# Sixteen-kilobyte runs and 4 MB loads for streamed expert weights

## The chip, the cores and the metric

The kernel runs on one core of a Trainium2 chip. The metric is the device time of one execution in microseconds (us). A core has the engines PE (TensorE), DVE (VectorE), ACT (ScalarE), POOL (GpSimd) and SP (SyncE), and 16 DMA engines that move data from the device memory to the core's own memory of 128 partitions.

## The reference, cut to what matters

One layer of a decoder for 256 tokens and 1024 channels: a mixer of three branches, then a feed-forward part of 32 experts of which each token takes four. The experts:

```python
def moe_ffn(h, router_w, router_b, w_gu, b_gu, w_down, b_down):
    logits = (t @ router_w + router_b).astype(jnp.float32)
    top_vals, top_idx = lax.top_k(logits, TOP_K)            # 4 of 32
    gate_w = jax.nn.softmax(top_vals, axis=-1)
    ...
    def expert_block(args):
        xb, e = args
        gu = xb @ w_gu[e] + b_gu[e]                         # w_gu[e]: 1024 x 2048, float32
        gate, up = jnp.split(gu, 2, axis=-1)
        gate = jnp.minimum(gate, SWIGLU_LIMIT)
        up = jnp.clip(up, -SWIGLU_LIMIT, SWIGLU_LIMIT)
        glu = gate * jax.nn.sigmoid(SWIGLU_ALPHA * gate)
        return ((up + 1.0) * glu) @ w_down[e] + b_down[e]   # w_down[e]: 1024 x 1024, float32
```

All weights are float32 and every expert is used: 268 MB of gate/up weights and 134 MB of down weights, each read once.

## The kernel before, in words

The mixer takes the first 335 us of the profiled execution, the routing some 9 us, and the experts nearly all of the rest. Experts are worked on in 16 pairs, 0 to 15. The tokens of a pair lie in the 128 columns of the array, in four groups of 32, so one product with a block of weights is four matmuls of 32 columns (`tiles4`, L1286 in the profile), which take their weights as the moving operand.

For pair p PE does gate/up p first, in eight blocks of 128 input channels (`gate_up`), and then down p-1 (`down`). Between blocks stand the scatter of an earlier pair's result (L1276), the gather of the next pair's tokens (L1121), and at the end of gate/up a bias product (L1303) and the transposes of the activations (`transpose_act`, L1253). The last pair is written out by itself (`ahead`, `meanwhile`): down 14, a branch on whether some expert has more tokens than slots (PE's sequencer at L1393), and down 15, cut in small pieces so that its last products and the final norm come late by little.

Weights come by one stream. All loads stand in one list (`add`) in the order of their use, and SP issues them in that order with `nc.sync.dma_start` (`load`, L159). They land in a ring of seven buffers of 2 MB (`ringp`, 16 KB on each partition); three loads of the first two pairs go to buffers that the mixer no longer needs (`EXTRA`). `issue` emits as many loads as fit the ring; `passed` says that a buffer's weights are used up. A load that takes a used buffer waits for the last matmul that reads it.

One load of gate/up is 2 MB: one block of 128 rows for both experts of the pair, 8 KB in one run to each partition, in one DMA. One load of down is 2 MB in two DMAs of 1 MB, one for each expert: two blocks of 128 rows, 4 KB in one run. Partition p holds row k * 128 + p of block k, so the channels of a block are 128 neighbours. Down 14 and 15 are loaded by columns, in pieces of 512 and 256 (runs of 2 KB and 1 KB).

Of the kernel before, what the change touches and what calls it, by code (L numbers as in the profile page):

```python
# [19 lines left out]
P = 128  # L20
# [29 lines left out]
class Carve:  # L50
    """Consecutive column ranges of a tile."""
# [11 lines left out]
class Turn:  # L63
    """Operands taken in turn."""
# [11 lines left out]
def trunk(ctx: ExitStack, tc: tile.TileContext, x, c, norm1_g, ada_w, ada_b, w_in, gmlp_norm_g, gmlp_ws,  # L76
# [6 lines left out]
    ringp = ctx.enter_context(tc.tile_pool(name="ring", bufs=RING))  # L83
# [31 lines left out]
    loads, got = [], []  # L115
    free_now = {}

    def add(fn, where=None):
        loads.append((fn, where))
        return len(loads) - 1  # L120

    def issue(n):
        """Emits the loads that fit while load n is in use and earlier ones are not."""
        while len(got) < len(loads):
            i = len(got)
            fn, where = loads[i]
# [14 lines left out]
    def chunk(n):  # L141
        """Load n; earlier ones are not used any more, but for those that are held."""
        last[0] = max(n, last[0])
        issue(min(held | {last[0]}))
        assert loads[n][1] or sum(loads[j][1] is None for j in range(n, len(got))) <= RING
# [3 lines left out]
    def passed(n):  # L149
        """Load n and those before it are not used any more."""  # L150
# [24 lines left out]
    def add_ada1(q):  # L175
        """Columns q*256 .. of shift1 and scale1."""
# [7 lines left out]
    def add_ada23(j):  # L184
        """512 columns of gate1, shift2, scale2, gate2."""
# [40 lines left out]
    EXTRA = {(0, KB - 1): "rest", (1, KB - 2): "b2", (1, KB - 1): "b4"}  # L226

    def add_gu(p, k):
        src = wgu[2 * p:2 * p + 2, k * P:(k + 1) * P, :].rearrange("e p n -> p e n")
# [7 lines left out]
        gu_ids[p, k] = add(fn, EXTRA.get((p, k)))  # L237

    def add_dn(p, *slots):
        """Loads of the pair's rows k0 .. k0 + k, columns c0 .. c0 + n, several to a slot."""  # L240
        dn_ids[p] = []

        def fn(t, parts):
            off = 0
            for k0, k, c0, n in parts:
                for e in range(2):
                    load(blocks(t, k, n, off=off), rows_of(wdn[2 * p + e], k0, k, c0, n))
                    off += k * n
        for parts in slots:
            i = add(lambda t, parts=parts: fn(t, parts))  # L250
# [5 lines left out]
    for p in range(NP):  # L256
        for k in range(KB):
            if (p, k) not in EXTRA or p == 0:
                add_gu(p, k)
            if (p, k) == (0, 3):  # L260
# [3 lines left out]
        if p:  # L264
            add_dn(p - 1, *([[(2 * q, 2, 0, D)] for q in range(4)] if p < NP - 1 else
# [4 lines left out]
    # ------------------------------------------------------------------ what stays  # L270
# [4 lines left out]
    vec2 = keep.tile([P, 64], F32, name="vec2")  # L275
    C_, N1, A1 = 0, 8, 16
    GG, PS_, CW, N2, A2 = 0, 8, 16, 40, 48
# [20 lines left out]
    vrow1, vrow2 = b4(P, rows=32), b4(P, rows=64)  # L298
# [3 lines left out]
    # -- loads that come before the stream  # L302
# [4 lines left out]
    def late_loads():  # L307
# [3 lines left out]
        vrows(vrow2, N2, norm2_g[0])  # L311
        vrows(vrow2, A2, ada_b[0, 3 * D:5 * D])
        load(wsr, gmlp_ws[0].rearrange("h t s -> t h s"))
        load(bsr, gmlp_bs.rearrange("o h t -> o (h t)"))
        load(rw, router_w[0].rearrange("(k p) e -> p k e", p=P))
# [16 lines left out]
    def rstd(r, m, w, table=False):  # L332
        """r = m ** -0.5, w columns (eps is in m), polished by a Newton step."""
# [9 lines left out]
    def table(f):  # L343
        """Has function f's table on the engine ahead of its use."""
# [5 lines left out]
    # ================================================================== token mixer  # L350
    # -- x's statistics and c
# [20 lines left out]
    def turn_x(b):  # L372
        """Blocks 2b and 2b + 1 of the normed rows, turned channel-major."""
# [7 lines left out]
    # -- conditioning: products by channel, summed over the partitions by a product with ones  # L381
# [10 lines left out]
    def weigh_rows(acc, w, k, first=False):  # L392
        """acc (+)= row block k of w times the conditioning."""
# [5 lines left out]
    def weigh_tiles(ps, w, i):  # L399
        """Products of the conditioning and w: row block g + 4i added in each of rows 32g .. 32g + 31, i = 0, 1."""  # L400
# [10 lines left out]

    def to_sums(acc, by):
        """Sums over the partitions that by picks: columns b * 128 .. of them in each of rows 32b .. 32b + 31."""
        ps = bbank()
        for b in range(4):
            TE.matmul(ps[b * GRP:(b + 1) * GRP, :P], lhsT=by[:, :1].to_broadcast([P, GRP]), rhs=acc[:, b * P:(b + 1) * P], start=True, stop=True)
# [26 lines left out]
    def h_block(kk):  # L443
        """Block kk of h, channel-major, as an exact pair."""
# [16 lines left out]
    def pair3(out_, ws, xs_, first, last_):  # L461
        """out_ += ws x xs_ for pairs (hi, lo) of both, without lo x lo (below float32's last bit)."""
# [7 lines left out]
    def col_item(name, m, pair, evac):  # L470
        """128 columns of a weight, channel-major."""
# [19 lines left out]
    def row_step(get, kk, banks, pair, evac, before=None):  # L491
        """One block of rows times 512 columns, token-major."""
# [22 lines left out]
    def later(k, fn):  # L515
        """Has fn emitted k steps later."""
# [5 lines left out]
    # -- v: gelu, root mean square over the channels  # L522
# [33 lines left out]
    # -- u, first with half of the channels, then with the rest  # L556
# [31 lines left out]
    def spatial_setup():  # L588
        """Spatial weights, transposed and causal; their bias on every partition; the other vectors."""
# [24 lines left out]
        def vectors():  # L614
            ps[2] = bbank()
            TE.transpose(ps[2][:, :64], vrow2, ident[:64, :64])

        def to_vec2():
            V.tensor_copy(vec2, ps[2][:, :64])
# [6 lines left out]
    def shift_scale(q, *between):  # L626
        """The rows of products, their sums by channel, and other steps after each."""
# [8 lines left out]
    def v_steps(q, *parts):  # L636
        """Columns c2 of row block k for parts (c2, k)."""
# [20 lines left out]
    # -- the spatial gate  # L658
# [17 lines left out]
    class Act:  # L676
        """The operand pair of the projections, made when the first part of it is."""
# [14 lines left out]
    # -- the other two thirds of the conditioning, a row block at a time between the steps  # L692
# [3 lines left out]
    def ada23(j):  # L696
# [27 lines left out]
        def cols_evac():  # L724
            u = 4 * (j - 2)
            V.tensor_tensor(mod2[:, u:u + 4], cell["pc"], vec2[:, A2 + u:A2 + u + 4], op=OP.add)
# [5 lines left out]
            if j == 5:  # L732
                V.scalar_tensor_tensor(a2, mod2[:, KB:], 1.0, vec2[:, N2:N2 + 8], op0=OP.add, op1=OP.mult)
# [16 lines left out]
    def gate_bias(j):  # L750
        """Rows of zeros, but for the bias on the first partition."""
# [19 lines left out]
    # -- gates and the first projection  # L771
# [739 lines left out]
```

## Time and profile before

| | us |
|---|---|
| median of 3 runs | 1311.47 |
| lowest, highest | 1308.33, 1312.13 |
| span of the profiled execution | 1308.2 |
| PE busy in it | 1201.0 |

The profiled execution is told by its span, from the first to the last instruction; what lies around the span is not in the trace, and the lowest of the runs stands at the span within 0.2 us. A timeline row has the start and the length of a group of equal instructions in us, then engine, line, operation, output and input, count, and in brackets the idle time before and what ended it. L1286 is line 1286 of the kernel. `SPq` rows are DMA issues on SP. `PEclk` is the share of TensorE's full clock that was granted, and the DMA share is the mean busy share of 16 DMA engines by their packets' time, which can come out a little above 1. 484.75 MB are moved in the whole execution.

### The profile page before, as it was taken

The numbers are of one execution on the slowest core, as the hardware profiler recorded it, in microseconds if no ns is written. First come the engines' busy times: TensorE is split into PE (matmuls) and PEld (weight loads), VectorE is DVE, ScalarE is ACT, GpSimd is POOL, SyncE is SP. The second block draws the span as 40 slices with busy tenths as digits, with TensorE's granted clock in tenths as the row PEclk, the third lists the DMA queues.
The fourth block names the chain that finished last, engine by engine and source line by source line (L and its number), as shares of the span: only waits on it lengthen the run. The fifth ranks groups of instructions, "written<-read, shape, count | busy, mean of one in ns | idle before, by whom it ended". The sixth has DMA issues, their size and how long they took to land. (4 is left out here: it accounts for less than half of the span.)

```text
span 1308.2 us, 22663 instructions
## 1 busy us (share of the span) xinstructions
PE 1201.0 (92%) x9653; PEld 603.3 (46%) x9654; DVE 440.1 (34%) x884; ACT 270.6 (21%) x538; POOL 11.0 (1%) x27
## 2 busy tenths in 40 slices
PE   7999999999899999999897999898888989898867
PEld 5899998999533333333232333232323323232222
DVE  3477886877431121311112221212111111212022
ACT  5564554555321010100000010100000000001002
POOL 0010000000000000000000000000000000000001
PEclk9999999999999999999999999999999999999989
DMA  9996487776999999999999999999999999999993
GB/s 344 340 387 223 179 293 292 264 277 264 329 390 368 418 417 414 420 413 420 413 421 413 420 414 418 417 416 418 414 420 414 420 414 418 416 419 416 387 366 117
DMA packets 121014, 484.75 MB, mean 371 GB/s; under 512 B 6601, under 2 KB 21033, under 8 KB 88398
## 3 DMA queue, kind: packets, MB, share of 16 engines
q1 hardware_dynamic: 120230, 481.52, 92.6%
q10 hardware_dynamic: 680, 1.71, 0.4%
q8 instruction: 81, 1.33, 0.4%
q14 instruction: 23, 0.19, 0.0%
HBM read 482.16 MB, written 1.05 MB: 369 GB/s over the span
## 5 line engine op out<-in xcount | busy, mean ns | idle before, releaser
L1286 PE MATMUL abank<-wchunk,b 128*32 (+2 forms) x4160 | 478.1, 592 | 52.9 <-DMA wchunk<-in_exp_w_down_dram 41.8
L1286 PEld LDWEIGHTS abank<-wchunk,b 128*32 128x32 f32 x4160 | 135.8, 110 | 359.9 <-issue 356.6
L1286 PE MATMUL cbank<-wchunk,b 128*32 128x512 f32 (+2 forms) x1952 | 231.9, 593 | 14.6 <-DMA wchunk<-in_exp_w_gu_dram 14.6
L1058 DVE TENSOR_SCALAR b<-bbank,a,mod 128x128 f32<-128x128 f32 x64 | 26.2, 410 | 398.6 <-PE bbank L1121 398.6
L458 DVE TENSOR_TENSOR spl<-wchunk,spl 128x512 fp32r<-128x512 f32 x196 | 132.2, 691 | 49.0 <-ACT spl L457 46.1
L1056 ACT ACTIVATE b<-bbank,mod,a 128x128 f32<-128x128 f32 x64 | 29.2, 457 | 540.5 <-PE bbank L1121 540.5
L457 ACT ACTIVATE spl<-wchunk 128x512 fp32r<-128x512 f32 x196 | 120.8, 627 | 76.3 <-PE abank L468 46.5
L465 PE MATMUL abank<-b,spl 128*128 128x256 f32 x432 | 110.3, 287 | 0.0
L466 PE MATMUL abank<-b,spl 128*128 128x256 f32 x432 | 108.3, 283 | 0.0
L1121 PEld LDWEIGHTS bbank<-spl,b 128*128 128x128 f32 x512 | 65.6, 191 | 91.2 <-issue 89.3
L1286 PEld LDWEIGHTS cbank<-wchunk,b 128*32 128x32 f32 x1952 | 51.6, 109 | 117.6 <-issue 85.9
L1121 PE MATMUL bbank<-spl,b 128*128 128x128 f32 x512 | 86.3, 298 | 2.0 <-DVE spl L1114 0.9
L465 PEld LDWEIGHTS abank<-b,spl 128*128 128x128 f32 x432 | 82.7, 192 | 3.5 <-issue 2.4
L1339 DVE TENSOR_TENSOR row<-abank,x 128x512 f32<-128x512 f32 (+1 forms) x32 | 21.9, 683 | 182.7 <-PE abank L1286 182.7
L466 PEld LDWEIGHTS abank<-b,spl 128*128 128x128 f32 x432 | 82.8, 192 | 0.2 <-issue 0.2
L1218 DVE TENSOR_TENSOR xt<-bbank,xt 128x512 f32<-128x512 f32 (+1 forms) x66 | 44.6, 676 | 106.0 <-PE bbank L1276 105.9
L468 PE MATMUL abank<-b,spl 128*128 128x256 f32 x432 | 69.7, 283 | 0.0
L1276 PE MATMUL bbank<-row,b 128*128 128x512 f32 (+1 forms) x132 | 62.7, 605 | 1.6 <-DVE row L1339 1.4
L468 PEld LDWEIGHTS abank<-b,spl 128*128 128x128 f32 x432 | 59.8, 192 | 0.0
L465 PE MATMUL cbank<-b,spl 128*128 128x256 f32 x224 | 57.2, 287 | 0.0
L466 PE MATMUL cbank<-b,spl 128*128 128x256 f32 x224 | 56.2, 283 | 0.0
L1269 ACT ACTIVATE b<-bbank 128x256 f32<-128x256 f32 x16 | 6.1, 383 | 237.5 <-PE bbank L1267 237.5
(272 smaller groups left out, 839.0 us busy)
## 6 DMA issues: line engine op xcount, KB each, us to landing
wchunk<-in_exp_w_gu_dram SPq DMA_DIRECT2D x125, 2048.0 KB, 22.9
wchunk<-in_exp_w_down_dram SPq DMA_DIRECT2D x122, 1024.0 KB, 27.0
wchunk<-in_w_in_dram SPq DMA_DIRECT2D x16, 2048.0 KB, 9.6
wchunk<-in_ada_w_dram SPq DMA_DIRECT2D x8, 2048.0 KB, 19.7
wchunk<-in_ada_w_dram SPq DMA_DIRECT2D x16, 512.0 KB, 14.7
wchunk<-in_exp_w_down_dram SPq DMA_DIRECT2D x10, 512.0 KB, 9.1
wchunk<-in_w_in_dram SPq DMA_DIRECT2D x4, 1024.0 KB, 10.1
wchunk<-in_w_proj_a_dram SPq DMA_DIRECT2D x2, 2048.0 KB
```

Source lines behind the costliest of these rows:

```text
L457: S.activation(hi, w, AF.Copy)
L458: V.tensor_tensor(lo, w, hi.bitcast(F32), op=OP.subtract)
L465: TE.matmul(out_, lhsT=wh, rhs=xh, start=first and i == 0, stop=False)
L466: TE.matmul(out_, lhsT=wh, rhs=xl, start=False, stop=False)
L468: TE.matmul(out_, lhsT=wl, rhs=xh, start=False, stop=last_ and i == n - 1)
L1056: S.activation(out_, in_, AF.Identity, scale=a2[:, k:k + 1], bias=sh2[:, k:k + 1])
L1058: V.tensor_scalar(out_, in_, a2[:, k:k + 1], sh2[:, k:k + 1], op0=OP.mult, op1=OP.add)
L1121: TE.matmul(ps, lhsT=xn2[:, tt, k * P:(k + 1) * P], rhs=oh[p][:, tt].rearrange("p a g -> p (a g)"), start=tt == 0, stop=tt == TT - 1)
L1218: V.tensor_tensor(xt[:, tt, s], ps, xt[:, tt, s], op=OP.add)
L1276: TE.matmul(ps, lhsT=wt[:, tt * P:(tt + 1) * P], rhs=wk["yv"][:, c:c + n], start=True, stop=True)
L1286: TE.matmul(out_[g * GRP:(g + 1) * GRP], lhsT=xl[:, g * GRP:(g + 1) * GRP], rhs=w(e), start=start, stop=stop, skip_group_check=True)
L1339: V.tensor_tensor(wk["yv"][:, c:c + m], bank[c], wk["g2b"][:, c:c + m], op=OP.mult)
```

## The change

A partition takes neighbouring rows of a weight: two of gate/up, four of down, 16 KB in one run of the device memory. The input channels of a block are then every second, or every fourth, channel, and all that meets the weights is read to match: the transposes of the activations take every fourth column, the transposes and sums of the mixer's result every second (`of_block`), the copies of the normed rows and the loads of three vectors and of the router's weights are reordered.

The ring is one buffer of seven units of 2 MB. Loads of gate/up and down are 4 MB, in two DMAs of 2 MB (one for each expert), and go to units 0 and 1, 2 and 3, or 4 and 5; unit 6 takes loads of 2 MB only: the mixer's, single blocks of the first two pairs, down 14 and 15. `lay` fixes beforehand which units a load takes, those whose last load is the oldest, and `issue` emits a load once all loads before it in its units are passed.

```diff
-    ringp = ctx.enter_context(tc.tile_pool(name="ring", bufs=RING))
+    ringp = ctx.enter_context(tc.tile_pool(name="ring", bufs=1))
...
+    ring = ringp.tile([P, RING * CHUNK_ELEMS], F32, name="wchunk")
...
+    def lay():
+        first = next(i for i, (_, _, size) in enumerate(loads) if size == 2)
+        turn = -sum(where is None for _, where, _ in loads[:first]) % RING
+        of = [-RING + (u - turn) % RING for u in range(RING)]
+        for i, (_, where, size) in enumerate(loads):
+            if where is not None:
+                place.append((None, ()))
+                continue
+            u = min(range(0, RING - size + 1, size), key=lambda u: max(of[u:u + size]))
+            place.append((u, tuple(j for j in of[u:u + size] if j >= 0)))
+            of[u:u + size] = [i] * size
...
             if where is None:
-                if sum(loads[j][1] is None for j in range(n, i)) >= RING:
+                u, before_it = place[i]
+                if any(j >= n for j in before_it):
                     return
-                t = ringp.tile([P, CHUNK_ELEMS], F32, name="wchunk")
+                t = ring[:, u * CHUNK_ELEMS:(u + size) * CHUNK_ELEMS]
...
-    EXTRA = {(0, KB - 1): "rest", (1, KB - 2): "b2", (1, KB - 1): "b4"}
+    EXTRA = {(0, KB - 2): None, (0, KB - 1): "rest", (1, KB - 2): "b2", (1, KB - 1): "b4"}
...
+    def add_gu2(p, j):
+        def fn(t):
+            v = t.rearrange("p (e m) -> p e m", e=2)
+            for e in range(2):
+                load(v[:, e], wgu[2 * p + e, 2 * j * P:2 * (j + 1) * P, :].rearrange("(p i) n -> p (i n)", i=2))
+        n = add(fn, None, 2)
+        for i in range(2):
+            gu_ids[p, 2 * j + i] = (n, i)
...
-            add_dn(p - 1, *([[(2 * q, 2, 0, D)] for q in range(4)] if p < NP - 1 else
+            add_dn(p - 1, *([[(4 * j, 4, 0, D)] for j in range(2)] if p < NP - 1 else
                             [[(k, 4, c, 512)] for c in (0, 512) for k in (0, 4)]))
...
-            S.activation(xn2[:, tt, half(h)], xt[:, tt, half(h)], AF.Copy, scale=r2[:, tt:tt + 1])
+            S.activation(xn2[:, tt, half(h)].rearrange("p (j i q) -> p j i q", j=2, i=2),
+                         xt[:, tt, half(h)].rearrange("p (j q i) -> p j i q", j=2, i=2), AF.Copy, scale=r2[:, tt:tt + 1])
...
-                kk = 4 * b + k
-                TE.transpose(ps[:, k * P:(k + 1) * P], a[:, kk * P:(kk + 1) * P], ident)
+                TE.transpose(ps[:, k * P:(k + 1) * P], a[:, half(b)].rearrange("p (q i) -> p i q", i=4)[:, k], ident)
...
-            if (p, k) not in EXTRA:
-                passed(gu_ids[p, k])
+            if EXTRA.get((p, k)) is None and row != 0:
+                passed(n)
```

How this moves the issues on SP, at pair 2's gate/up and the start of down 1. A row is a DMA with its output, input and shape; `PE_49` in brackets is a wait for a count of PE's (the last matmul that reads the buffer's former weights), `DMAHW0_49` to `DMAHW7_49` the wait for the DMA eight places earlier in one of eight lanes. Before:

```order
L159 DMA wchunk<-in_exp_w_gu_dram 128x2x2048 [waits DMAHW6_49,PE_49]
L159 DMA wchunk<-in_exp_w_gu_dram 128x2x2048 [waits DMAHW7_49,PE_49]
L159 DMA wchunk<-in_exp_w_down_dram 128x2x1024 [waits DMAHW0_49,PE_49]
L159 DMA wchunk<-in_exp_w_down_dram 128x2x1024 [waits DMAHW1_49]
```

These are the last two blocks of gate/up and the two DMAs of the first down load. And now, from the first load of gate/up 2 to the end of down 1:

```order
L176 DMA wchunk<-in_exp_w_gu_dram 128x4096 [waits DMAHW5_49,PE_49]
L176 DMA wchunk<-in_exp_w_gu_dram 128x4096 [waits DMAHW6_49]
L176 DMA wchunk<-in_exp_w_gu_dram 128x4096 [waits DMAHW7_49,PE_49]
L176 DMA wchunk<-in_exp_w_gu_dram 128x4096 [waits DMAHW0_49]
L176 DMA wchunk<-in_exp_w_gu_dram 128x4096 [waits DMAHW1_49,PE_49]
L176 DMA wchunk<-in_exp_w_gu_dram 128x4096 [waits DMAHW2_49]
L176 DMA wchunk<-in_exp_w_gu_dram 128x4096 [waits DMAHW4_49,DMAHW3_49,PE_49]
L176 DMA wchunk<-in_exp_w_gu_dram 128x4096 [waits DMAHW6_49]
L176 DMA wchunk<-in_exp_w_down_dram 128x4096 [waits DMAHW7_49,DMAHW5_49,PE_49]
L176 DMA wchunk<-in_exp_w_down_dram 128x4096 [waits DMAHW0_49]
L176 DMA wchunk<-in_exp_w_down_dram 128x4096 [waits DMAHW1_49,PE_49]
L176 DMA wchunk<-in_exp_w_down_dram 128x4096 [waits DMAHW2_49]
```

Each load of 4 MB is two DMAs of 2 MB with one wait for PE between the two; a load waits for PE once where two loads of gate/up waited each for its own. PE, DVE, ACT and POOL have as many instructions as before.

## Rows read from the trace of the kernel before

**Rows 1.** The page: busy time of PE; DMA packets.

```profile
PE 1201.0 (92%) x9653; PEld 603.3 (46%) x9654; DVE 440.1 (34%) x884; ACT 270.6 (21%) x538; POOL 11.0 (1%) x27
DMA packets 121014, 484.75 MB, mean 371 GB/s; under 512 B 6601, under 2 KB 21033, under 8 KB 88398
```

**Rows 2.** Waits of PE, 424 to 1246 us: total, times, longest.

```profile
PE abank L1286 <- DMA wchunk<-in_exp_w_down_dram: 40.8, 29, 1.5
...
PE cbank L1286 <- DMA wchunk<-in_exp_w_gu_dram: 14.6, 18, 1.3
```

**Rows 3.** Stretches: length, PE, PEld, DVE, ACT, POOL busy (count); PEclk, DMA share, GB/s.

```profile
64.00:96.00 32.00, 31.39 (x244) 29.04 (x243) 22.46 (x46) 22.37 (x49) 3.66 (x8) 1.00 1.05 387
452.00:467.00 15.00, 15.00 (x132) 5.31 (x128) 0.96 (x3) 0.56 (x2) 0.00 (x0) 1.00 1.03 409
909.00:922.00 13.00, 13.00 (x108) 4.15 (x106) 2.38 (x5) 0.46 (x1) 0.00 (x0) 1.00 1.01 422
979.00:989.00 10.00, 10.00 (x92) 3.53 (x86) 0.41 (x1) 0.46 (x1) 0.00 (x0) 1.00 1.01 420
999.00:1010.00 11.00, 9.63 (x88) 3.51 (x84) 5.48 (x9) 1.72 (x3) 0.00 (x0) 1.00 1.03 411
416.00:420.00 4.00, 3.96 (x34) 1.77 (x38) 3.87 (x7) 2.62 (x5) 0.00 (x0) 1.00 0.86 316
421.00:424.00 3.00, 3.00 (x36) 0.91 (x32) 0.11 (x1) 0.00 (x0) 0.00 (x0) 1.00 0.50 128
424.00:428.00 4.00, 4.00 (x44) 1.23 (x40) 0.00 (x0) 0.00 (x0) 0.00 (x0) 1.00 1.01 428
1246.00:1256.00 10.00, 3.84 (x34) 1.12 (x32) 5.07 (x8) 1.26 (x2) 0.00 (x0) 1.00 1.04 382
1256.00:1266.00 10.00, 4.11 (x20) 1.15 (x24) 0.42 (x1) 0.00 (x0) 0.00 (x0) 0.51 1.05 377
```

**Rows 4.** DMA issues of gate/up weights: count, size, median us to landing.

```profile
wchunk<-in_exp_w_gu_dram SPq DMA_DIRECT2D x125, 2048.0 KB, 22.9
```

**Rows 5.** Timeline of SP: single issues of gate/up 2 and of down 1.

```profile
421.17 0.37 SPq L159 DMA_DIRECT2D wchunk<-in_exp_w_gu_dram  x1
...
424.61 0.37 SPq L159 DMA_DIRECT2D wchunk<-in_exp_w_gu_dram  x1
...
445.21 0.88 SPq L159 DMA_DIRECT2D wchunk<-in_exp_w_down_dram  x2
```

**Rows 6.** Timeline of PE: down 0 and gate/up 2; later starts of gate/up.

```profile
417.47 13.94 PE L1286 MATMUL abank<-wchunk,b 128*32 x128
...
432.89 1.29 PE L1253 MATMUL bbank<-ident,b 128*128 128x128 f32 x8
434.12 1.92 PE L1286 MATMUL cbank<-wchunk,b 128*32 x16
...
437.69 3.90 PE L1276 MATMUL bbank<-row,b 128*128 128x512 f32 x8
...
488.70 1.92 PE L1286 MATMUL cbank<-wchunk,b 128*32 x16
...
964.71 1.92 PE L1286 MATMUL cbank<-wchunk,b 128*32 x16
...
1024.88 1.92 PE L1286 MATMUL cbank<-wchunk,b 128*32 x16
```

**Rows 7.** Timeline of PE: last block of gate/up 15, first product of down 14.

```profile
1241.90 1.92 PE L1286 MATMUL cbank<-wchunk,b 128*32 x16 [1.31 <-DMA wchunk<-in_exp_w_gu_dram]
...
1247.29 3.64 PE L1286 MATMUL abank<-wchunk,b 128*32 x32 [1.08 <-DMA wchunk<-in_exp_w_down_dram]
```

**Rows 8.** Timeline of ACT (routing; late mixer) and of SP (late mixer).

```profile
343.64 0.46 ACT L1056 ACTIVATE b<-bbank,mod,a 128x128 f32<-128x128 f32 x1 [3.18 <-PE bbank L1121]
...
253.42 6.76 SPq L159 DMA_DIRECT2D wchunk<-in_w_out_dram  x2
...
270.70 0.63 ACT L457 ACTIVATE spl<-wchunk 128x512 fp32r<-128x512 f32 x1 [0.48 <-PE abank L468]
```

More of the change, by code (lines that the diff above doesn't have):

```diff
@@ L110, in bbank, with add @@
         return psb.tile([P, 512], F32, name="bbank")
-    loads, got = [], []
+    loads, got, place = [], [], []
     free_now = {}
-    def add(fn, where=None):
-        loads.append((fn, where))
+    ring = ringp.tile([P, RING * CHUNK_ELEMS], F32, name="wchunk")
+    def add(fn, where=None, size=1):
+        loads.append((fn, where, size))
         return len(loads) - 1
+    def lay():
[9 more added lines that the diff above has]
+            of[u:u + size] = [i] * size
     def issue(n):
+        if not place:
+            lay()
         while len(got) < len(loads):
             i = len(got)
-            fn, where = loads[i]
+            fn, where, size = loads[i]
             if where is None:
-                if sum(loads[j][1] is None for j in range(n, i)) >= RING:
+                u, before_it = place[i]
+                if any(j >= n for j in before_it):
                     return
-                t = ringp.tile([P, CHUNK_ELEMS], F32, name="wchunk")
+                t = ring[:, u * CHUNK_ELEMS:(u + size) * CHUNK_ELEMS]
             else:
@@ L144, in chunk @@
         issue(min(held | {last[0]}))
-        assert loads[n][1] or sum(loads[j][1] is None for j in range(n, len(got))) <= RING
         assert n < len(got)
@@ L236, in fn, with dn_rows @@
                 c += v.shape[2]
-        gu_ids[p, k] = add(fn, EXTRA.get((p, k)))
+        gu_ids[p, k] = (add(fn, EXTRA[p, k]), None)
+    def dn_rows(w, k0, k, c0, n):
+        j, i = k0 // 4, k0 % 4
+        v = w[4 * j * P:4 * (j + 1) * P]
+        if (k, n) == (4, D):
+            return v.rearrange("(p i) n -> p (i n)", i=4)
+        return v[:, c0:c0 + n].rearrange("(p i) n -> p i n", i=4)[:, i:i + k]
     def add_dn(p, *slots):
@@ L246, in fn @@
                 for e in range(2):
-                    load(blocks(t, k, n, off=off), rows_of(wdn[2 * p + e], k0, k, c0, n))
+                    v = t[:, off:off + k * n]
+                    load(v if (k, n) == (4, D) else v.rearrange("p (k n) -> p k n", k=k), dn_rows(wdn[2 * p + e], k0, k, c0, n))
                     off += k * n
         for parts in slots:
-            i = add(lambda t, parts=parts: fn(t, parts))
+            size = sum(2 * a[1] * a[3] for a in parts) // CHUNK_ELEMS
+            i = add(lambda t, parts=parts: fn(t, parts), None, size)
             off = 0
@@ L256, in trunk @@
     for p in range(NP):
[L257 to L260, printed above, removed]
+        for j in range(KB // 2):
+            if (p, 2 * j) not in EXTRA:
+                add_gu2(p, j)
+            elif p == 0:
+                for i in range(2):
+                    add_gu(p, 2 * j + i)
+            if (p, j) == (0, 1):
                 for pk_ in EXTRA:
@@ L274, in trunk @@
     vec1 = keep.tile([P, 32], F32, name="vec1")
-    vec2 = keep.tile([P, 64], F32, name="vec2")
+    vec2 = keep.tile([P, 40], F32, name="vec2")
+    vec3 = keep.tile([P, 24], F32, name="vec3")
     C_, N1, A1 = 0, 8, 16
-    GG, PS_, CW, N2, A2 = 0, 8, 16, 40, 48
+    GG, PS_, CW = 0, 8, 16
+    N2, A2 = 0, 8
     mod1 = keep.tile([P, 2, KB], F32, name="mod1")
@@ L297, in trunk @@
     hfs = Turn([b4(T) for _ in range(2)])
-    vrow1, vrow2 = b4(P, rows=32), b4(P, rows=64)
+    vrow1, vrow2 = b4(P, rows=32), b4(P, rows=40)
     bsr = b4.t[:1, 8 * T:8 * T + D]
@@ L1309, in gate_up @@
         for i, k in enumerate(in_turn(p)):
-            t = chunk(gu_ids[p, k])
+            n, row = gu_ids[p, k]
+            t = chunk(n)
             ws = []
@@ L1313, in gate_up @@
                 v = v.rearrange("p (e n) -> p e n", e=2)
+                if row is not None:
+                    v = v[:, :, row * 2 * FF:(row + 1) * 2 * FF]
                 ws.extend(v[:, :, c:c + 512] for c in range(0, v.shape[2], 512))
@@ L1370, in spill @@
         for k in range(KB):
-            load(wt_, wgu[bass.ds(e, 1), k * P:(k + 1) * P, :].rearrange("o p n -> p (o n)"))
+            j, i = divmod(k, 2)
+            load(wt_, wgu[bass.ds(e, 1), 2 * j * P:2 * (j + 1) * P, :].rearrange("o (p i) n -> p i (o n)", i=2)[:, i])
             for b in range(4):
@@ L1379, in spill @@
             w = blocks(wt_, 2, D)
-            load(w, wdn[bass.ds(e, 1), 2 * q * P:(2 * q + 2) * P, :].rearrange("o (k p) n -> p (o k) n", p=P))
+            j, i = q // 2, 2 * (q % 2)
+            load(w, wdn[bass.ds(e, 1), 4 * j * P:4 * (j + 1) * P, :].rearrange("o (p i) n -> p (o i) n", i=4)[:, i:i + 2])
             for k in range(2):
```

24 lines of the change are left out of this document (14 added, 10 removed).

## Prediction

> **What bounds the kernel now.** I read the page's engine table and packet counts first, then the waits of PE, then stretches by engine. TensorE is busy for 92% of the span [rows 1], which looks like a TensorE kernel; but that is an average over two stages with different limits. Up to about 344 us (the token mixer) TensorE has work all the time while the transfers have gaps. In the expert stage it is the other way round: between 424 and 1246 us PE waits 40.8 us for down weights and 14.6 us for gate/up weights, nearly always 1.3 to 1.5 us at a time [rows 2], one wait for each 2 MB of weights. The stretches say the same: the DMA engines are busy for the whole of every one (share 1.01 to 1.03) [rows 3]. So from the middle of the stage on the weight stream sets the end, and TensorE catches up with every load.
>
> How fast the stream runs goes with the length of a run. The 2 KB runs of the mixer's weights move 387 GB/s, the 4 KB runs of the down weights 409 and 411, the 8 KB runs of the gate/up weights 422 and 420 [rows 3]. A run is a packet as far as 8 KB: the page counts 121014 - 88398 = 32616 packets of 8 KB or more [rows 1], and 125 gate/up loads of 2048 KB [rows 4] make 125 x 256 = 32000 runs of 8 KB.
>
> **The rate term.** With 16 engines busy, a packet takes 16 x size / rate: 84.7 ns for 2 KB (387), 159.8 ns for 4 KB (410), 311.3 ns for 8 KB (421). Each further 2 KB costs 75.1 to 75.8 ns, so about 9.3 ns belong to the packet and not to its bytes. An estimate for 16 KB, from those rows, is 311.3 + 4 x 75.6 = 613.7 ns, or 427 GB/s. Bounds: no gain beyond 8 KB, 421; no cost of a packet left at all, 8192 x 16 / 302.4 ns = 433. The one free stretch after the stream's restart shows 428 with 8 KB runs [rows 3], so 427 is not out of reach. A slower 16 KB run is not excluded by any row either; I keep it with the rivals.
>
> A pair of experts has 16.777 MB of gate/up and 8.389 MB of down weights. Gate/up: 39.85 us at 421, 39.28 at 427.1, so -0.57. Down: 20.46 us at 410, 19.64 at 427.1, so -0.82. That is -1.39 us a pair. Thirteen pairs are streamed with the stream as the limit in both kernels (gate/up 3 to 15, down 1 to 13): -18.1. The last 12.58 MB of gate/up 2 gain another 0.43. Down 14 and 15 keep their pieces of 2 KB and 1 KB. Together **-18.5 us** (bounds: at 421 only the down loads gain, 0.53 x 13 = -6.9; at 433 it is -26).
>
> **The ring term.** The ring keeps seven units of 2 MB, but loads of 4 MB use six of them, as three slots. What matters is the last time that the ring was full and the stream stood still, since from there on it runs through. Before, that is at 420 to 423 us: the engines run down to 0.50 of their time [rows 3], with the ring full (three blocks of gate/up 2 and four of down 0). The first of the four loads of down 0 is used up 3.5 us (13.94 / 4) after 417.47, and SP issues the next load at 421.17; data flow at the full rate from about 423.4 [rows 3, 5, 6], 2.2 us after the issue. In the changed kernel the next load is blocks 2 and 3 of gate/up 2. It wants the whole first half of down 0, which ends at the second issue of before, 424.61 [rows 5]: 3.44 us later. And where the old ring held three blocks of gate/up 2 at that moment, the new one holds two, so one 2 MB unit more is still to come: 2.097 MB / 421 = 4.98 us. That makes +8.4. Once more in that pair the stream runs dry: the load of blocks 6 and 7 waits until blocks 0 and 1 are used up, 445.21 in the trace of before (there the next down load [rows 5]), while what is on its way ends at 426.85 + 2 x 9.82 = 446.5; with 2.2 us until data flow that is a gap of about +1. Sum **+9.4**. Bounds: +5 if the later issue is made up (one unit only), +14 if gate/up 3 meets such gaps too.
>
> After that I take no gap. PE needs 54.6 us for a pair when nothing is late (434.12 to 488.70) [rows 6], the stream 39.3 + 19.6 = 58.9, so PE catches up within two or three pairs. In the steady state, counted from the landing of the last half of a down block (T0): PE is done with it 7.0 us later (half of 13.94 [rows 6]), and releases that slot for load three of the next pair; gate/up blocks 0 and 1 land at T0 + 9.8, are used by T0 + 9.8 + 2 x 3.64 (a block [rows 7]) + 3.9 (the scatter between them [rows 6]) = T0 + 21.0, and release their slot while the two loads behind them run until T0 + 29.4. The tightest release thus has 8.4 us of queued data ahead of it, against the 2.2 us that a restart costs. Each first DMA of a load waits for PE, the second only for its lane, as the order of SP's instructions shows; nothing but weight loads is queued on SP behind them.
>
> **The tail term.** Before, the last 2 MB of gate/up 15 let PE start at 1241.90, and down 14 starts 5.39 us later, at 1247.29, having waited 1.08 us for its data [rows 7]. Then everything is on chip early and PE alone sets the rest; down 14 and 15 are unchanged. The rest is a block of 3.64 us and the bias products, 0.67. After, 4 MB land together, and PE has two blocks and the bias products before down 14: 8.0 us instead of 5.39, so **+2.6**; the data of down 14 are there by then.
>
> **The edits that compensate for the new row order.** The strided reads of the transposes, the strided copies of the second norm on ACT and the loads of three vectors in runs of 8 bytes cost 0 in my sum. Eight transposes take 1.29 us in one group [rows 6]; doubled, two groups at the end would give +2.6, the bound above; elsewhere they lie in a wait for data. The copies have 3.18 us in which ACT stands idle behind them [rows 8]. The vector loads fall in the mixer, where the stream has slack. No reason for a gain, so the low bound is 0. By the new rule for slots the mixer's loads gC1, pC0 and pC1 are issued only where wo0 is, at 253.42; the first step that reads one of them stands at 270.70 [rows 8], time enough for a load of 2 MB that runs some 5 us, so 0.
>
> **Sum.** -18.5 + 9.4 + 2.6 = -6.5 us on a span of 1308.2, so 1301.7. The median of the runs is 1311.47, 3.3 us above that span; on its scale the forecast is **1305**.
>
> **The Trainium skill.** Its page "HBM Reference", section Specifications (TRN2), says that a core that streams alone measures about 425 GB/s, bounded by its 16 DMA engines. By that the pair would gain 1.15 us, 14.9 in all, and the sum would be about -2.9: no change that can be told. The trace has 428 GB/s in one stretch of 4 us, so it doesn't quite agree, but it has no longer stretch above 422. [...]
>
> **Rivals.** (A) The longer run gains nothing: the engines cut runs above 8 KB, or 8 KB is already at the limit. Then the down loads alone gain 6.9, the ring and the tail still cost 12.0: +5.1, 1316.5. For it: the step from 4 to 8 KB already brought only 11 GB/s. It turns slower than before where 16 KB runs move less than about 423.6 GB/s, the rate at which the saving is 12.0. Chance 0.15. (B) The limit lies near 425: -2.9, about 1308.5, within the noise. Chance 0.2. (C) Three coarse slots starve the stream in every pair: a release would have to come more than 27 us after T0 instead of 21, for instance if the loads' landing lags behind their bytes by several us on some engines. Each pair would then pay 1 to 2 us, +13 to +26 over the forecast: 1318 to 1331. Against it: 8.4 us of cover. Chance 0.07. (D) The packet's own cost goes, 431 to 433 GB/s: 1293.5 to 1298. Chance 0.18. (E) PE now waits 2.8 us at a time instead of 1.4. In the tail the granted clock fell to 0.51 after a stretch in which PE was busy 3.84 of 10 us [rows 3]; 2.8 of 9.8 us leaves PE busy far longer than that, and while the stream is the limit a slow block is absorbed by the next wait. It prices at +1.5 at the tail, within my range.
>
> **How the numbers follow.** The forecast itself (a saving of 15 to 21 us, net -3 to -10) has 0.4. A change under 0.3%, 3.9 us, can't be told here. Faster: the forecast's larger part 0.36, D 0.18, a few hundredths of B: 0.56. Same: B, and the edges of the forecast and of A: 0.25. Slower: most of A, C, and what I overlooked in the ring: 0.19. The range for 8 in 10 is 1294 to 1317; it takes in A and most of D and leaves out C. The forecast's own range is 1300 to 1309.
>
> **What would show it.** The stretches of the steady pairs: 427 GB/s or more with a DMA share of 1.0, in gate/up and in down alike, and a pair of about 58.9 us instead of 60.2 (964.71 to 1024.88 before [rows 6]). A packet count near 16 KB for the expert weights (an estimate from the counts of loads: some 37,000 packets fewer) shows that runs aren't cut. The restart: SP's issue at about 424.6, and a second short dip near 446. PE's waits half as many and twice as long. The tail: about 8 us from the last gate/up landing to down 14. Wrong it would be with stretches at 421 or less, with a DMA share under 0.98 at pair edges after 650 us, or with a new wait of PE on ACT or DVE behind the strided reads.

## The result, and the profile after

The changed kernel takes 1300.16 us (median of 4 runs, 1298.93 to 1302.01), the one before 1311.8 beside it: a ratio of 0.9919, 95% interval 0.9905 to 0.9933. It is faster, by 11.6 us where the forecast said 6.5, inside its range. Part of that is the four runs of the kernel before: with more runs, beside the experiments, its median was 1309.69 to 1309.93 us, and against that the change is worth 9.5 to 9.8. The profiled executions stand nearer to the forecast: the span went from 1308.2 to 1300.3, by 7.9 us.

The page of the changed kernel (busy time, slices of DMA share left out, packets), to set beside [rows 1]:

```profile
PE 1211.8 (93%) x9653; PEld 613.4 (47%) x9654; DVE 439.8 (34%) x884; ACT 270.8 (21%) x538; POOL 11.0 (1%) x27
...
DMA packets 83765, 484.73 MB, mean 373 GB/s; under 512 B 6753, under 2 KB 21161, under 8 KB 59854
```

The same bytes go in 37249 packets fewer; the estimate was some 37,000, with runs of 16 KB kept whole. The waits of PE, 424 to 1246 us (total, times, longest), beside [rows 2]:

```profile
PE abank L1336 <- DMA wchunk<-in_exp_w_down_dram: 31.9, 19, 2.7
...
PE cbank L1336 <- DMA wchunk<-in_exp_w_gu_dram: 10.6, 11, 2.5
```

Fewer waits, and longer: 30 instead of 47, up to 2.7 us instead of 1.5, as one load now feeds PE for two blocks. Stretches of the changed kernel, columns as in [rows 3]:

```profile
342.00:345.00 3.00, 2.09 (x13) 1.93 (x12) 1.66 (x10) 0.00 (x0) 0.00 (x0) 0.76 1.07 223
345.00:348.00 3.00, 3.00 (x24) 1.01 (x26) 0.24 (x1) 0.46 (x1) 0.00 (x0) 0.68 0.80 190
424.00:429.00 5.00, 5.00 (x52) 1.53 (x48) 0.00 (x0) 0.00 (x0) 0.00 (x0) 1.00 0.47 132
446.00:450.00 4.00, 4.00 (x40) 1.42 (x36) 0.41 (x1) 0.00 (x0) 0.00 (x0) 1.00 0.93 336
450.00:456.00 6.00, 6.00 (x56) 1.85 (x48) 0.00 (x0) 0.46 (x1) 0.00 (x0) 1.00 0.95 390
500.00:513.00 13.00, 13.00 (x113) 4.47 (x116) 1.75 (x4) 0.46 (x1) 0.00 (x0) 1.00 1.01 426
540.00:550.00 10.00, 8.53 (x64) 2.68 (x64) 0.56 (x1) 0.00 (x0) 0.00 (x0) 0.83 1.01 426
560.00:572.00 12.00, 12.00 (x105) 3.85 (x104) 1.73 (x4) 0.46 (x1) 0.00 (x0) 1.00 1.01 429
745.00:750.00 5.00, 4.79 (x19) 1.74 (x22) 4.14 (x7) 0.00 (x0) 0.00 (x0) 0.66 1.01 433
750.00:755.00 5.00, 5.00 (x48) 1.68 (x44) 0.00 (x0) 0.46 (x1) 0.00 (x0) 1.00 0.85 357
755.00:760.00 5.00, 5.00 (x49) 1.70 (x44) 0.41 (x1) 0.00 (x0) 0.00 (x0) 1.00 0.64 206
```

In two stretches of the steady pairs the stream runs at 426 and 429 GB/s, where 427 was forecast. Stretches of 10 us scatter, so a long one says more; 285 us of gate/up and down, first before and then after:

```profile
460.00:745.00 285.00, 266.04 (x2128) 90.87 (x2124) 63.48 (x113) 22.88 (x44) 0.00 (x0) 0.99 1.02 417
```

```profile
460.00:745.00 285.00, 265.03 (x2098) 92.41 (x2090) 59.30 (x107) 22.89 (x44) 0.00 (x0) 0.98 1.01 427
```

After the change the stream stands still for about half of 424 to 429, while the ring is full, dips a little near 450 as foretold, and dips once more at 750 to 760, which was not foretold. The first two rows of the longer table show TensorE's granted clock falling between its two levels (2.4 and 1.2 GHz) at the start of the experts; before, it stayed at 1.00 there.

The places of the ring term and of the tail, PE's timeline (as in [rows 6, 7]):

```profile
420.08 13.94 PE L1336 MATMUL abank<-wchunk,b 128*32 x128
...
1235.59 1.93 PE L1336 MATMUL cbank<-wchunk,b 128*32 x16 [2.48 <-DMA wchunk<-in_exp_w_gu_dram]
...
1243.26 3.64 PE L1336 MATMUL abank<-wchunk,b 128*32 x32
1254.08 5.71 PE L1336 MATMUL abank<-wchunk,b 128*32 x32 [7.18 <-PEq L1448]
```

and SP's issues of gate/up 2 (two DMAs to a load), beside [rows 5]:

```profile
427.22 0.80 SPq L176 DMA_DIRECT2D wchunk<-in_exp_w_gu_dram  x2
...
447.92 0.80 SPq L176 DMA_DIRECT2D wchunk<-in_exp_w_gu_dram  x2
```

From four points that both traces have, the start of down 0, the landing of the last gate/up load (1241.90 and 1235.59), the start of down 14 and the end, the difference can be laid out:

| stretch | before | after | difference | forecast |
|---|---|---|---|---|
| start to down 0 | 417.47 | 420.08 | +2.6 | 0 |
| down 0 to the last gate/up load landed | 824.43 | 815.51 | -8.9 | -9.1 (rate -18.5, ring +9.4) |
| from there to down 14 | 5.39 | 7.67 | +2.3 | +2.6 |
| down 14 to the end | 60.9 | 57.0 | -3.9 | 0 |
| span | 1308.2 | 1300.3 | -7.9 | -6.5 |

### The profile page after: what moved, and what is told of

The parts are those of the page before. It is cut to its first block, busy times and chain, and to the rows that moved or that the text cites. A ratio compares the mean times of both kernels' runs of the same rounds, so it can differ in the third digit from the quotient of the medians.

```text
span 1300.3 us, 22561 instructions
## 1 busy us (share of the span) xinstructions
PE 1211.8 (93%) x9653; PEld 613.4 (47%) x9654; DVE 439.8 (34%) x884; ACT 270.8 (21%) x538; POOL 11.0 (1%) x27
## 5 line engine op out<-in xcount | busy, mean ns | idle before, releaser
L1336 PE MATMUL abank<-wchunk,b 128*32 (+2 forms) x4160 | 485.6, 603 | 39.1 <-DMA wchunk<-in_exp_w_down_dram 31.9
L1336 PEld LDWEIGHTS abank<-wchunk,b 128*32 128x32 f32 x4160 | 139.8, 112 | 349.4 <-issue 322.4
L1336 PE MATMUL cbank<-wchunk,b 128*32 128x512 f32 (+2 forms) x1952 | 231.6, 592 | 10.7 <-DMA wchunk<-in_exp_w_gu_dram 10.6
## 6 DMA issues: line engine op xcount, KB each, us to landing
wchunk<-in_ada_w_dram SPq DMA_DIRECT2D x8, 2048.0 KB, 11.9
wchunk<-in_exp_w_down_dram SPq DMA_DIRECT2D x10, 512.0 KB, 12.4
wchunk<-in_w_in_dram SPq DMA_DIRECT2D x4, 1024.0 KB, 10.7
```

Of the source, the lines that this page charges most:

```text
L1336: TE.matmul(out_[g * GRP:(g + 1) * GRP], lhsT=xl[:, g * GRP:(g + 1) * GRP], rhs=w(e), start=start, stop=stop, skip_group_check=True)
```

## The experiments

Profiles are compared by spans where a few us matter: the runs behind a median lie 2 to 8 us apart. Each kernel has one profile. The first eight runs and the last four (from the later down bias on) were on two different chips, each with the kernel before beside it.

**Short runs in the new loads.** The two sources of a load get rows 128 apart:

```diff
-                load(v[:, e], wgu[2 * p + e, 2 * j * P:2 * (j + 1) * P, :].rearrange("(p i) n -> p (i n)", i=2))
+                load(v[:, e].rearrange("p (i n) -> p i n", i=2), wgu[2 * p + e, 2 * j * P:2 * (j + 1) * P, :].rearrange("(i p) n -> p i n", i=2))
...
-            return v.rearrange("(p i) n -> p (i n)", i=4)
+            return v.rearrange("(i p) n -> p i n", i=4)
...
-                    load(v if (k, n) == (4, D) else v.rearrange("p (k n) -> p k n", k=k), dn_rows(wdn[2 * p + e], k0, k, c0, n))
+                    load(v.rearrange("p (k n) -> p k n", k=k), dn_rows(wdn[2 * p + e], k0, k, c0, n))
```

> The changed kernel with its 4 MB loads, its three slots and its order, but the runs cut back: a partition takes rows 128 apart (8 KB runs of gate/up, 4 KB runs of down), so that products meet other rows of the weights than in the reference. Theory (length of a run): the stream falls back to about 421 and 410 GB/s, and the whole rate term of 18.5 us comes back while ring and tail stay as they are after the change: 1300.2 + 18.5 = about 1318.7, slower than before. Rival (fewer and larger loads bring the gain, whatever their runs): it stays near 1300.

Measured: 1322.21 us, ratio 1.0107 (1.0088 to 1.0125), span 1319.9. The page counts 121141 packets, and two stretches (gate/up, then down; columns as above) are back at the old rates:

```profile
560.00:572.00 12.00, 12.00 (x87) 3.86 (x89) 3.50 (x6) 0.46 (x1) 0.00 (x0) 1.00 1.01 419
588.00:600.00 12.00, 11.35 (x100) 4.64 (x100) 5.48 (x9) 2.18 (x4) 0.00 (x0) 1.00 1.03 409
```

The span grows by 19.6 us against the changed kernel, 18.5 expected; in the stretch where runs should matter, from down 0 to the landing of the last gate/up load, it is 19.1 (834.65 and 815.51). By medians the step is 22.1 us and by the two ratios some 24.6, so the size is known to about 5 us. Large loads without long runs gain nothing; with the ring's cost they are slower than the kernel before. The rival falls.

**Short runs for down alone** (the second and third hunk above).

> The same for the down weights alone: runs of 4 KB there, gate/up stays at 16 KB; products of down meet other rows of the weights. Theory: 0.82 us a pair by 13 pairs = 10.7 us come back: about 1311. Down stretches at 410 GB/s, gate/up at 427. Rival (larger loads): near 1300. If runs matter only above some amount of traffic, something between.

Measured: 1314.19 us, ratio 1.0038 (1.0023 to 1.0052), span 1311.7, 11.4 above the changed kernel, 10.7 expected. By the two ratios the step is 15.6, so its size is known to some 4 us; that the down weights carry more than half of the rate term holds either way.

**A ring of six units in the kernel before**, the very last load in a buffer of its own.

```diff
-RING = 7
+RING = 6
...
+            i = add(lambda t, parts=parts: fn(t, parts), "wlast" if p == NP - 1 and parts is slots[-1] else None)
```

> The kernel before with a ring of six units instead of seven (the very last load has a buffer of its own), everything else as before: the ring term's first part alone. Theory: when the ring is full at about 421 us one 2 MB unit less has been loaded, and the stream, which sets the end from there, has 2.097 MB / 421 GB/s = 5.0 us more: about 1311.8 + 5.0 = 1316.8. Rival (TensorE bounds the early pairs and catches up, the ring's last unit is worth nothing): 1311.8.

Measured: 1315.4 us, ratio 1.0054 (1.0031 to 1.0077). In the profile everything up to 488 us stands as before within 0.2 us, and the last gate/up block, at 1241.90 before, is late by 4.8:

```profile
1246.69 1.50 PE L1286 MATMUL cbank<-wchunk,b 128*32 x12 [1.31 <-DMA wchunk<-in_exp_w_gu_dram]
```

By medians it is 5.7 slower than the kernel before beside it. A unit of the ring is worth about the time of its bytes, once.

**Seven units in a circle, first try** (two of the changed places).

```diff
+            us = [(at + k) % RING for k in range(size)]
...
+                    v = ring.rearrange("p (u m) -> p u m", u=RING)[:, lo:hi + 1:hi - lo]
```

> The changed kernel, but loads of 4 MB take the next two units of a circle of seven, neighbours or units 6 and 0 (then the DMAs go in the order in which these units come free): all seven units work, and the first half of a load needn't wait for the unit of the second. Theory: the unit that lay idle is worth 5.0 us, the earlier issue of half a load up to 3.4 more: 1300.2 - 5.0 to 8.4 = 1292 to 1295. Rival (the ring costs nothing, only the rate counts): 1300.

Measured: 1454.6 us, ratio 1.1117. Both theories missed: PE now waits up to 18 us at a time for loads (waits of PE, 340 us to the end):

```profile
PE cbank L1350 <- DMA wchunk<-in_exp_w_gu_dram: 65.1, 4, 17.5
PE cbank L1350 <- DMA wchunk<-in_exp_w_down_dram: 52.4, 3, 17.7
PE abank L1350 <- DMA wchunk<-in_exp_w_gu_dram: 36.1, 3, 18.1
```

The view of a load in units 6 and 0 spans the whole ring, so such a load may count as touching all units between, and PE would wait for loads that it doesn't read. No run shows this by itself; the next kernel, without such loads, has no wait of PE for a load above 3.3 us. The run says nothing of the ring's worth.

**Seven units, no load at both ends.**

```diff
+    def wraps():
+        return sum(size for _, where, size in loads if where is None) % RING == RING - 1
...
+        if wraps():
+            for i in range(2):
+                add_gu(p, 2 * j + i)
+            return
...
+            u = at % RING
+            at += size
```

The loads of down are split in the same way (left out here).

> The changed kernel with a plain circle of seven units: a 4 MB load takes the next two, and a load that would take unit 6 and unit 0 is made as two loads of 2 MB with 8 KB runs instead. (The circle before this one let such a load lie in both ends; its PE then waited up to 18 us for loads that it doesn't read.) Theory: the idle unit is worth 5.0 us, the earlier issue of a load's first DMA up to 3.4 more, the twelve or so pieces with 8 KB runs cost about 2: 1300.2 - 3 to 6.4 = 1294 to 1297. Rival (the ring's size and grain cost nothing, as the stream could run ahead anyway): 1300 to 1302.

Measured: 1297.51 us, ratio 0.9905 (0.9884 to 0.9925), span 1295.9. By spans it is 4.4 better than the changed kernel, as expected; by ratios the intervals overlap. From down 0 to the start of the last gate/up block it takes 813.5 us where the changed kernel takes 819.0. The dip at 755 is gone:

```profile
750.00:755.00 5.00, 5.00 (x48) 2.08 (x48) 0.09 (x1) 0.46 (x1) 0.00 (x0) 1.00 1.00 416
755.00:760.00 5.00, 5.00 (x48) 1.69 (x44) 0.32 (x1) 0.46 (x1) 0.00 (x0) 1.00 1.02 423
```

**The fine tail**: the last 4 MB of gate/up as two blocks.

```diff
-    EXTRA = {(0, KB - 2): None, (0, KB - 1): "rest", (1, KB - 2): "b2", (1, KB - 1): "b4"}
+    EXTRA = {(0, KB - 2): None, (NP - 1, KB - 2): None, (NP - 1, KB - 1): None, (0, KB - 1): "rest", (1, KB - 2): "b2", (1, KB - 1): "b4"}
```

> The changed kernel, with the last 4 MB of gate/up 15 alone as two loads of 2 MB, one for each block (8 KB runs): undoes the tail term. Theory: PE has one block less to do after the last gate/up weights land, -2.3 us as the trace after shows it (7.67 us from there to down 14 instead of 5.39), +0.1 for the shorter runs: about 1298. Rival (what follows, the branch and the final stretch, absorbs it): 1300.

Measured: 1301.36 us, ratio 0.9929 (0.9908 to 0.995), span 1297.3. In the trace down 14 starts at 1240.82 instead of 1243.26, 2.4 earlier, having waited for its data again:

```profile
1240.82 3.64 PE L1336 MATMUL abank<-wchunk,b 128*32 x32 [0.75 <-DMA wchunk<-in_exp_w_down_dram]
```

The term is there in the trace; the medians don't show it, with an interval of 5.5 us.

**Seven units and fine tail.**

> Both of these together. Theory: they add, 1291.5 to 1295. Rival: the gain of the ring is lost again at the tail: as the circle alone.

Measured: 1295.69 us, ratio 0.9884 (0.9865 to 0.9904), span 1295.1: the best ratio of all, and the only one whose interval lies below the changed kernel's, by little.

**The branch in the last pair.** The forecast left the time after down 14 as it was; it fell by 3.9 us, nearly all of it where PE stands at the branch, 10.96 us before and 7.18 after (`PEq L1448` above). PE's timeline before:

```profile
1261.89 5.83 PE L1286 MATMUL abank<-wchunk,b 128*32 x32 [10.96 <-PEq L1393]
```

The branch's instructions on PE, before and then after: engine, operation, count, shortest/median/longest in ns.

```profile
L1393 PEldq COMPARE_BRANCH  x2: 5132/6190/7249, 1248.6 to 1254.1; - x2
```

```profile
L1448 PEldq COMPARE_BRANCH  x2: 385/3306/6226, 1244.6 to 1247.3; - x2
```

The first of two branch instructions takes 0.4 us instead of 5.1. One run asked why, and three more below bear on it. It shifts the code behind pair 4:

```diff
+            if i == 0 and 4 <= p < 12:
+                tiles4(pg[0], xs[p % 2][:, k], lambda e: of_expert(ws[0], e, slice(0, 512)), sel[p], True, False)
```

> The kernel before with 16 more matmuls in the first block of gate/up in each of pairs 4 to 11 (they repeat the first four tiles; the result is not touched), 128 in all, at places where PE waits for weights: the code behind them, with the branch in the last pair, stands elsewhere in memory. In the trace of before the branch's two instructions on PE took 5.1 and 7.2 us, in the changed kernel and two of its variants 0.4 and 6.2. Theory (their time depends on where the code lies, not on the weight stream): they change by several us in one direction or the other, and the rest stays within 1 us. Rival (the stream's state at the branch decides, a fetch waits behind queued weights of the same amount): 5.1 and 7.2 as before, and the total is 1310 as before.

Measured: 1311.56 us, ratio 1.0008 (0.9996 to 1.002). (The trace counts 64 more matmuls: one `tiles4` is 8, not 16.) The two instructions took 6.2 and 5.5 us: each changed, their sum hardly. Neither theory decided.

**The down bias later**, for the dip at 755:

```diff
-            if k == 1 and p == 7:
-                bias_down()
...
+            if k == KB - 1 and p == 7:
+                bias_down()
```

> The changed kernel with one piece of PE work moved: the down bias of all pairs (L1281, 5 to 7 us of PE, once, in gate/up 7 after its second block) now comes after the last block of that gate/up. In the trace of the changed kernel the stream runs dry once in the steady part, by 2.4 us at 750 to 760 us, when that work delays the release of the slot of blocks 2 and 3; with seven units, and in the kernel before, it doesn't. Theory (three coarse slots have too little cover for one delay of 7 us): the dip at 755 goes, the last gate/up lands 2.4 us earlier, about 1297.8. Rival (the stream had slack there, or another release comes late instead): 1300.

Measured: 1301.6 us, ratio 0.9934 (0.9919 to 0.995). The dip at 755 is gone, but others stand behind it, and nothing is won:

```profile
755.00:760.00 5.00, 3.73 (x36) 1.46 (x36) 0.55 (x2) 0.00 (x0) 0.00 (x0) 1.00 1.00 426
780.00:785.00 5.00, 5.00 (x52) 1.44 (x48) 0.00 (x0) 0.00 (x0) 0.00 (x0) 1.00 0.83 318
```

The rival was right: with three slots another release comes late instead. The granted clock falls at the new place of the bias too:

```profile
770.00:775.00 5.00, 4.79 (x19) 1.39 (x22) 4.89 (x9) 0.63 (x1) 0.00 (x0) 0.58 1.02 433
```

**Eight products in the routing's wait**, on seven units and fine tail:

```diff
-WARM = [8,0,4,0,2]
+WARM = [8,8,4,0,2]
```

> Seven units, the fine tail, and eight products that nobody reads while PE waits in the routing, before 341 us. In all kernels with the new layout the granted clock fell to 0.5 to 0.76 at 342 to 348 us, in those with the old one it stayed at 1.0, and the first products took 0.7 to 2 us longer; the next full ring starts moving by as much later. Theory (an idle stretch of 1.4 us of PE just before lets it fall): it stays at 1.0, down 0 starts 1 to 2 us earlier and so does all that follows: about 1294. Rival (it falls for another reason, or the delay is made up by the ring): 1295.7, with the clock as before.

Measured: 1297.18 us, ratio 0.9903 (0.9888 to 0.9918), span 1293.2. The clock stays at 1.00 where it was 0.60 and 0.50 without these products, and 0.76 and 0.68 in the changed kernel (stretches):

```profile
342.00:345.00 3.00, 2.03 (x19) 1.36 (x21) 1.54 (x7) 0.46 (x1) 0.00 (x0) 1.00 1.04 236
345.00:348.00 3.00, 3.00 (x33) 0.69 (x21) 0.00 (x0) 0.00 (x0) 0.00 (x0) 1.00 0.70 175
```

Against the same kernel without these products, down 0 starts 2.8 us earlier (418.25, 421.09) and the last gate/up block 3.8 earlier (1228.52, 1232.33). Most of it was lost again at the branch, where PE stands for 10.54 us instead of 7.08:

```profile
L1465 PEldq COMPARE_BRANCH  x2: 5580/5944/6309, 1234.9 to 1241.5; - x2
```

**The same with the code where it was**: `WARM = [4,4,4,0,2]`.

> Seven units and the fine tail again, with four of the eight products that nobody reads at the kernel's start moved into the routing's wait, so that PE's program is as long as without them and the branch's code stands where it did. In the run before, eight added there held the clock at 1.0 and brought down 0 forward by 2.8 us and the last gate/up landing by 3.8 us, but the branch's two instructions on PE went from 0.5 and 6.1 us to 6.3 and 5.6. Theory (the branch's time depends on where its code lies): 0.5 and 6.1 here, the clock at 1.0, and the end 2 to 4 us before the 1295.7 of seven units and fine tail: 1292 to 1294. Rival (the earlier stream or the clock made the branch slower): 6 and 5.6 here too, about 1297.

Measured: 1295.0 us, ratio 0.9894 (0.9874 to 0.9914), span 1291.1, the shortest of all; by medians it can't be told from the kernel without the moved products. Down 0 starts at 417.60, as early as in the kernel before (417.47). The branch is short again:

```profile
L1465 PEldq COMPARE_BRANCH  x2: 477/3313/6149, 1235.6 to 1238.3; - x2
```

The loads are those of the run before, the stream is as early (its last gate/up block within 0.9 us), and the branch has its short time: an early stream alone did not make it long, as far as one profile of each can tell.

**The kernel before, with eight products more**: `WARM = [8,8,4,0,2]`.

> The kernel before, with eight products that nobody reads added in the routing's wait of 1.45 us (some 1.8 us of PE, at most 0.4 late): PE's program grows by as much as in the run that made the branch slow in the new layout, and by that its length is again that of the changed kernel. Theory (position of the code): the branch's two instructions take about 0.4 and 6.2 us instead of 5.1 and 7.2, and the kernel before ends some 3.8 us earlier without any change to its loads: about 1306. Rival (the new layout's loads themselves make the branch short): 5.1 and 7.2, about 1310.

Measured: 1309.3 us, ratio 0.9992 (0.998 to 1.0004). The branch keeps its time:

```profile
L1393 PEldq COMPARE_BRANCH  x2: 4837/6026/7214, 1248.9 to 1254.1; - x2
```

This prediction failed: an equal length of PE's program (19514 of PE's instructions recorded before the branch, 19516 in the changed kernel) doesn't make the branch short in the old kernel. What stays: sixteen matmuls in front of it turned 0.5 us into 6.3 in one kernel with the same loads, so the program in front of it counts.

The traces show what PE stands for there. The page counts the transfers that bring instructions to the engines:

```profile
q8 instruction: 81, 1.33, 0.4%
```

They are 16 KB each. In nine kernels of the fourteen the first branch instruction takes 0.4 to 1.0 us, and none of these transfers starts within it. In the other five (the kernel before, its ring of six, its two forms with products added, and the new one with eight products added) it takes 4.8 to 6.3 us, and one of them starts 2.3 to 3.7 us after its beginning. The second branch instruction, 5.5 to 7.2 us everywhere, always has at least one. So the long branch goes with a fetch of instructions at that moment. For which engine a transfer is, the trace doesn't say, and why an old kernel with a program of equal length has its fetch within the branch stays open.

## Why the prediction was right, and where not

The rate, ring and tail terms hold in kind, and nearly in size. That the span came out within 1.4 us of the forecast is also luck: two steps taken at 0 were off by 2.6 and -3.9, and a dip that was not foreseen is hidden in the stretch that fits best (-8.9 for -9.1).

**The rate term** was right in kind, and somewhat small. Its estimate for a 16 KB run, 427 GB/s from the costs of 2, 4 and 8 KB runs, is what the stretches show (426 to 429, and 427 over 285 us). Cutting the runs back cost 19.6 us of span against 18.5, and more by medians. Rival A (nothing beyond 8 KB) falls. So does rival B (a limit near 425): by rate alone it is close, but it gave the term 14.9 us. The rule on a core that streams alone gives 425 in the Trainium skill's page "HBM Reference", section Specifications (TRN2), a little under what this stream holds. Rival D's 431 to 433 isn't reached.

Three readings of the prediction don't hold, and change little. At 433 its own sum gives a term of -29, not -26. At 425 a pair gains 1.10 us, not 1.15, and the trace of before does have stretches of 10 us above 422 (424 at 660 to 670 us). And PE doesn't wait once for each 2 MB: 47 waits [rows 2] stand against some 160 loads of 2 MB, so it catches up with the stream a few times in a pair.

**The ring term** was right in its steps. The load of blocks 2 and 3 goes out 7.14 us after down 0's start (420.08 to 427.22) where before one went out 3.70 after it (417.47 to 421.17): 3.44 later, as worked out. One unit less is worth 4.8 in the old kernel (4.98 forecast). The second dip is there: 0.6 us of stream by the DMA share, 1.3 by the bytes that were not moved, instead of 1.

**"After that I take no gap"** was wrong once, and by one of the prediction's own signs of being wrong: the DMA share fell under 0.98 after 650 us. At 750 to 760 us about 2.5 us of stream are lost by the share (0.15 and 0.36 of 5 us), some 3 by the bytes, where PE does the down bias between blocks of gate/up 7. The prediction looked at the release after blocks 0 and 1 in an ordinary pair, and missed the one pair with more work: there blocks 2 and 3 take 15.2 us, bias included, instead of 8.4 in the next pair, and their slot comes free 6.8 us later. Of these, 5.5 are the bias, and most of the rest comes from the clock (0.66 at 745 to 750). The kernel before has the same bias and the same fall of the clock, and so has the circle of seven units (0.69 and 0.63 at 740 to 750), and in both the stream runs on; before, the row is:

```profile
735.00:740.00 5.00, 4.59 (x16) 1.62 (x18) 4.51 (x8) 0.00 (x0) 0.00 (x0) 0.73 1.01 423
```

So the cover of three slots is thinner than the 8.4 us taken; an estimate from these numbers is 6.8 + 2.2 (the restart) - 2.5 = 6.5 us. It is rival C in small: once, not in every pair. The stretch came out right even so. With 19.1 for the rate, all ring costs in it together are 10.2; the steps named here add up to 11.3 to 12.5, and the 1 to 2 us between are not assigned.

**The tail term** (+2.6) was right: +2.3, and undoing it gave 2.4 back in the trace.

**The start** was taken at 0 and is +2.6. About 1 us lies in the first 45 us of the mixer (the same matmul starts at 44.04 and 45.03), and varies between profiles: one product of the routing starts at 340.29 before, at 341.41 after, and anywhere between 340.4 and 341.3 in the other kernels of the new layout. The other 1.4 us come between 341 and 350 us, where the clock is low; from there to down 0 nothing is added. It passes to the end in full, because the ring's restart waits for down 0: the prediction priced the edits of that stage by their own engines' slack and not by when PE frees the ring. Why the clock falls in all kernels with the new layout and in none with the old is open. PE's wait just before is as long in both (1.45 and 1.44 us), so the wait alone doesn't explain it; but products in that wait keep the clock at 1.00, and with four of them moved there down 0 starts as early as before.

**The end** was taken as unchanged and is -3.9, by the branch, whose first instruction no longer has a fetch of instructions in it. Nothing in the forecast pointed to that. The other 3.7 us of the difference in medians are the place of the two profiled executions among their runs: a run's time is 1.7 us above its span (1302.01 with the span of 1300.3), so the one before took some 1309.9, which is 1.9 below its median, and the one after lies 1.85 above. That the lowest run before stands at the span within 0.2 us, as said ahead of the prediction, is chance.

Rival E's lower clock in longer waits is there (a mean granted clock of 0.984 instead of 0.992, 0.83 at 540 to 550 us) and mostly absorbed: the stream beside it stays at 426 GB/s and a share of 1.01. No new wait on ACT or DVE behind the strided reads appears in the expert stage.

## What to carry to other kernels

When a stream of loads sets the end, price a new run length by the cost of a packet, fitted over the lengths that the trace already has. Then price the buffer: what is lost is counted from the last moment at which the ring stood full, in bytes that are not yet on chip and in the lateness of the first release. Look there also for the one pair with extra work, which three large slots did not cover. Larger loads cost once more at the very end, where the engine has more left to do after the last landing. A circle that uses every unit takes back part of the first cost (4.4 us of span here), and small loads at the end take back the second (2.4 in the trace; the medians don't show it).

## What the runs showed of the hardware that was not expected

The two branch instructions that every engine runs cost PE between 6.5 and 12.4 us, and the other engines under 0.1 us each; sixteen matmuls more in front of them moved the sum from 6.6 to 11.9 with the same loads, and with the longer time goes a fetch of instructions within the branch.

Transposes that read every fourth column take 1.38 us for eight instead of 1.29 [rows 6], a far smaller price than the doubling taken as a bound. The weight loads of these transposes take half as long again, 209 ns instead of 140, and the eight together grow by 0.09 us only (shortest/median/longest in ns, before and then after):

```profile
L1253 PEld LDWEIGHTS bbank<-ident,b x128: 137/140/143, 416.1 to 1268.4; 128*128 128x128 f32 x128
```

```profile
L1303 PEld LDWEIGHTS bbank<-ident,b x128: 195/209/219, 418.6 to 1260.5; 128*128 128x128 f32 x128
```

And a wait of 1.4 us filled with products that nobody reads kept TensorE's granted clock at 1.00 from 338 to 352 us, worth 2.8 us at the next point where the ring is full.
